# A decoder layer in fp32 split in two parts: in the first stage ScalarE makes the fp32 scaling of the input, and VectorE makes all lower parts of the index and query weights

## The chip, the cores and the metric

The kernel runs on one core of a Trainium2 chip. The metric is the device time of one execution in microseconds; the kernel before has a median of 1292.34 us over three runs (1291.21 to 1293.01). The engines are TensorE (PE in the profile, its weight loads PEld), VectorE (DVE), ScalarE (ACT) and GpSimd (POOL); SyncE (SP) issues every DMA.

## What is computed

One decoder layer over 1024 tokens and 1024 channels. What matters here is its beginning:

```python
mod = silu(c) @ w_mod + b_mod          # shift1, scale1, gate1, shift2, scale2, gate2
h = x * (1.0 + scale1) + shift1
proj = h @ w_in                        # columns [q | k | v | u | iq | ik | iw]
q, k, iq, ik = rope(q), rope(k), rope(iq), rope(ik)
score[t, s] = sum_h iw[t, h] * relu(iq[t, h] . ik[s])   # causal, s <= t
# the 256 keys of highest score are kept for each token; attention runs on those
```

Attention, a pooling branch, an output projection, two layer norms and a SwiGLU follow. The change does not touch them.

## The kernel before, in words

Every large matrix product is made with operands split in two: a higher part, which is the value rounded to the format that TensorE multiplies, and a lower part, which is the rest. Three products (high x high, high x low, low x high; `SPLITS`, line 293, in `mm_k`, line 295) stand for one. So each operand of 128x1024 costs two passes: `split` (line 276) has ScalarE copy the higher part out of a raw fp32 buffer and another engine subtract it from the raw buffer to give the lower part. That engine is VectorE unless `lo_eng` names GpSimd (`G`).

**First stage (loop over j, line 331).** The input is held with channels on partitions, in eight pieces of 128 channels, `xt` (128x1024, one column per token). For each piece j the loop loads two rows of `w_mod` (`wm`, two halves), has VectorE form scale1 and shift1 of its channels with two dot products of 128x1024 (`dot`, line 327) and two small additions, and then makes the two parts of h for these channels, `hT[j]`: ScalarE writes the higher part (line 349); a second instruction writes the scaled fp32 value back over `xt` (line 350); VectorE subtracts the one from the other for the lower part (line 351). At even j the next quarter of the index-query weights is split into `WS[j // 2]` (line 353). Then TensorE adds the products of this piece into seven open accumulators: index queries of token tiles 2 to 6 (`iq`, 15 matmuls a piece) and index keys and weights (`ik`, 6 matmuls a piece). Tile 7 is projected beside them by 24 matmuls named `pj`.

**Second stage, up to the scores.** ScalarE takes the index queries out of PSUM (`iq_take`), VectorE rotates tile 2 and the keys (`rope_tok(V, ...)`, line 456, and a rope on the transposed keys before it), and GpSimd rotates tiles 3 to 7 (line 466), three instructions of 128x512 a tile. Meanwhile the query weights take the place of the index-query weights in the same four buffers `WS[0..3]`: lines 457 to 463 split them, before with GpSimd for the lower parts of `WS[0]` and `WS[2]`, VectorE for `WS[1]` and `WS[3]`. TensorE projects query tile 0 with them (`pj`, four pieces of six matmuls; the first two pieces use `WS[0]` and `WS[1]`, the last two `WS[2]` and `WS[3]`), transposes the rotated tile 2 (`qT`) and the keys (`ikT`), and then starts the score products `lg` of tile 2. Scores of a tile are the eight heads' `lg`, a ReLU by ScalarE, and a weighted sum by VectorE (`score_X`). Query tile after query tile is projected between them. GpSimd rotates each projected query tile (`rope_V`) and masks the score tiles.

The raw weights go through a ring of three buffers (`RAW`, line 235). A load of the next raw piece waits until both parts of the old one have been made.

**What sets the order.** In these stages the framework's scheduler puts the instructions of each engine in an order from its own estimates; after this the instructions are kept in program order. Each engine works its list in order, so that an instruction that waits holds up all those behind it. SyncE's list of loads is in the order of the program.

Of the kernel before, what the change touches and what calls it, by code (L numbers as in the profile page):

```python
# [17 lines left out]
AF = mybir.ActivationFunctionType  # L18
ALU = mybir.AluOpType
# [54 lines left out]
def f_(ap):  # L74

    return ap.bitcast(F32)
# [110 lines left out]
def decoder_layer_kernel(  # L187
# [8 lines left out]
    V, A, G, T, SP = (Queue(tc, e, n, pinned, times) for e, n in  # L196
                      ((nc.vector, "V"), (nc.scalar, "A"), (nc.gpsimd, "G"), (nc.tensor, "T"), (nc.sync, "S")))
# [13 lines left out]
    def buf(where, off, n, name, dt=F32):  # L211
        return nc.alloc_sbuf_tensor_at(f"{name}_{where}{off}", [P, n], dt, offset=area[where] + 4 * off).ap()
# [21 lines left out]
    WS = [buf("W", k * 2048, 2048, "ws", F32R) for k in range(4)]  # L234
# [37 lines left out]
    def raw_slot():  # L272
        n_raw[0] += 1
        return RAW[(n_raw[0] - 1) % 3]

    def split(dst, raw, n, lo_eng=None):
        A.activation(dst[:, 0:n], raw, AF.Copy)
        (lo_eng or V).tensor_tensor(dst[:, n : 2 * n], raw, f_(dst[:, 0:n]), ALU.subtract)
# [6 lines left out]
    def hh(k, lo, t0, n):  # L285
        b = 1024 if lo else 0
        return hT[k][:, b + t0 : b + t0 + n]

    def ww(k, lo, c0, n):
        b = (1024 if lo else 0) + (k % 2) * 512  # L290
        return WS[k // 2][:, b + c0 : b + c0 + n]
# [3 lines left out]
    def mm_k(ps, lhs, rhs, ks):  # L295

        for k in ks:
            for m, (a, b) in enumerate(SPLITS):
                T.matmul(ps, lhs(k, a), rhs(k, b), start=(k == 0 and m == 0), stop=(k == KT - 1 and m == 2))
# [23 lines left out]
    def wikk(k, lo):  # L323
        b = (576 if lo else 0) + k * 72
        return wik[:, b : b + 72]

    def dot(wm, col):

        V.tensor_tensor_reduce(wm, wm, srow, 1.0, 0.0, ALU.mult, ALU.add, col)

    for j in range(KT):
        wm = wmr[j % 3]
        for hf in range(2):
            SP.dma_start(wm[:, hf * 1024 : (hf + 1) * 1024], wma_in[j][:, hf * 1024 : (hf + 1) * 1024])
        xt = xtr[j % 7]
        SP.dma_start(xt, xT_in[j])
        if j == 0:
            SP.dma_start(bcol, bcol_in)
        if j % 2 == 0:
            raw_iq = raw_slot()  # L340
            SP.dma_start(raw_iq, wiq_in[j // 2])
        if j == 0:
            SP.dma_start(wik_raw, wikw_in)
        mj = m1[:, 2 * j : 2 * j + 2]
        for hf in range(2):
            dot(wm[:, hf * 1024 : (hf + 1) * 1024], mj[:, hf : hf + 1])
        V.tensor_tensor(mj, mj, bcol[:, 2 * j : 2 * j + 2], ALU.add)
        V.tensor_scalar(mj[:, 0:1], mj[:, 0:1], 1.0, None, ALU.add)
        A.activation(hT[j][:, 0:1024], xt, AF.Identity, bias=mj[:, 1:2], scale=mj[:, 0:1])
        V.tensor_scalar(xt, xt, mj[:, 0:1], mj[:, 1:2], ALU.mult, ALU.add)  # L350
        V.tensor_tensor(hT[j][:, 1024:2048], xt, f_(hT[j][:, 0:1024]), ALU.subtract)
        if j % 2 == 0:
            split(WS[j // 2], raw_iq, 1024, G if j else V)
        if j == 0:
            split(wik, wik_raw, 576)
        for t in range(2, 7):
            mm_k(psq[t], lambda k, a: hh(k, a, t * P, P), lambda k, b: ww(k, b, 0, 512), [j])
        for c in range(2):
            mm_k(psk[c][0:72, :], lambda k, b: wikk(k, b), lambda k, a: hh(k, a, c * 512, 512), [j])
# [54 lines left out]
    raws = {}  # L414
# [40 lines left out]
                        float(np.float32(8.0 ** -0.5)), None, ALU.mult)  # L455
    rope_tok(V, iq_raw(2), iqtmp, 2)
    for kp in range(3):
        split(WS[kp], raws[kp], 1024, V if kp == 1 else G)
    raws[3] = raw_slot()
    SP.dma_start(raws[3], wq_in[3])  # L460
    for i in range(3, 7):
# [1415 lines left out]
```

## Time and profile before

| | |
|---|---|
| median of three runs | 1292.34 us |
| the profiled execution's own time | 1293.41 us |
| its span from first to last instruction | 1291.6 us |
| mean granted TensorE clock | 0.972 of full speed |
| busy: PE, DVE, ACT, POOL | 1200.3, 994.8, 654.5, 722.5 us |
| first stage: index-query products of the last piece end | about 63.5 us |
| first score product | 86.58 us |

Timeline rows read: start in us, length in us, engine, source line, operation, written tile <- read tiles, shapes, count, and in brackets the idle time of the engine just before and what ended it. Nearly all instructions have line L174, a helper that records every operation, so tiles tell them apart. A length of a merged row covers all its instructions. Matmul ends are modelled; the spacing of starts is the better measure, and PEld rows (weight loads, one per matmul) show it well.

### The profile page before, as it was taken

Reading aid. Unit: us, or ns where it says so; the run is one execution under the profiler, and the core shown is the slowest. Engines: PE = TensorE matmul, PEld = TensorE weight load, DVE = VectorE, ACT = ScalarE, POOL = GpSimd, SP = SyncE. Lnnn points to the kernel's source line nnn. Section 1 sums busy time; section 2 is a strip of 40 time slices with the busy share of each in tenths; the row PEclk is TensorE's granted clock in tenths of the full one; section 3 lists DMA queues with packets and bytes.
Section 4 is the critical chain, followed back from the end, with each engine's and each line's share of the span. In section 5 each row is a group of like instructions: output and inputs, shape, how many; then the busy total and the mean of one; then the engine's idle time right before and its main releaser. Section 6 shows DMA issues by size and latency. Waiting matters only on the chain.

```text
span 1291.6 us, 16411 instructions
## 1 busy us (share of the span) xinstructions
PE 1200.3 (93%) x5622; PEld 932.2 (72%) x5622; DVE 994.8 (77%) x1845; ACT 654.5 (51%) x1343; POOL 722.5 (56%) x510
## 2 busy tenths in 40 slices
PE   7979999999879999997799999999999999999996
PEld 6656565687646666886678787878888787878775
DVE  6758998877979866568687778687877777687798
ACT  3346878797668687265443333343433333333531
POOL 1383375657012355267666657483847566576848
PEclk9989999999958999999899999999999999999998
DMA  9510048521000016300111021201121110203112
GB/s 350 200 72 17 10 159 321 196 82 57 17 1 17 9 50 214 129 9 9 65 66 66 33 82 34 82 33 66 33 65 39 60 66 33 90 33 107 49 66 114
DMA packets 32460, 103.40 MB, mean 80 GB/s; under 512 B 3573, under 2 KB 3573, under 8 KB 28793
## 3 DMA queue, kind: packets, MB, share of 16 engines
q1 hardware_dynamic: 32376, 102.36, 22.5%
q8 instruction: 44, 0.72, 0.2%
q14 instruction: 40, 0.32, 0.1%
HBM read 92.90 MB, written 9.45 MB: 79 GB/s over the span
## 4 chain that ended last, share of the span: by engine, by line
PE 60%; DVE 18%; POOL 9%; issue 7%; ACT 5%; DMA 1%; SPq 0%; DVEq 0%; POOLq 0%; ACTq 0%
PE gu L174 24%; PE dn L174 14%; PE pj L174 5%; PE wo L174 4%; PE pair L174 3%; PE s L174 2%; PE pT L174 2%; PE o L174 2%; DVE act_W L174 2%; DVE score_X L174 2%; POOL wraw_R L174 2%; DVE junk_X L174 2%; PE lg L174 2%; DVE utmp_X L174 1%; POOL ws_W L174 1%
## 5 line engine op out<-in xcount | busy, mean ns | idle before, releaser
L174 PE MATMUL gu<-hr_H,wblk_T 128*128 128x512 f32 (+1 forms) x924 | 217.5, 388 | 6.1 <-ACT gtmp_V L174 2.7
L174 PE MATMUL gu<-hr_H,wblk_V 128*128 128x512 f32 (+1 forms) x924 | 215.8, 385 | 4.3 <-POOL wblk_V L174 2.1
L174 PEld LDWEIGHTS gu<-hr_H,wblk_T 128*128 128x128 f32 x924 | 172.2, 191 | 42.4 <-POOL wblk_T L174 3.6
L174 PEld LDWEIGHTS gu<-hr_H,wblk_V 128*128 128x128 f32 x924 | 169.9, 188 | 41.4 <-POOL wblk_V L174 4.2
L174 DVE TENSOR_TENSOR res_X<-res_X,dn 128x512 f32<-128x512 f32 (+1 forms) x253 | 159.0, 679 | 15.4 <-PE dn L174 15.3
L174 PE MATMUL pj<-ws_W,hT_H 128*128 128x512 f32 x456 | 117.3, 406 | 8.8 <-POOL ws_W L174 6.7
L174 POOL TENSOR_TENSOR wraw_R<-wraw_R 128x512 f32<-128x512 f32 x64 | 94.6, 1486 | 47.0 <-DVE wblk_T L174 23.7
L174 POOL TENSOR_TENSOR wraw_W<-wraw_W 128x512 f32<-128x512 f32 x60 | 86.9, 1456 | 59.6 <-DVE wblk_V L174 29.3
L174 POOL TENSOR_SCALAR sm_H<-sm_H,stat_X 128x1024 f32<-128x1024 f32 (+7 forms) x64 | 48.0, 764 | 124.1 <-DVE stat_X L174 96.0
L174 PEld LDWEIGHTS pj<-ws_W,hT_H 128*128 128x128 f32 x456 | 85.0, 192 | 33.2 <-POOL ws_W L174 7.0
L174 PE MATMUL dn<-wblk_T,act_W 128*128 128x512 f32 x324 | 78.8, 391 | 4.3 <-DVE act_W L174 4.3
L174 PE MATMUL dn<-wblk_V,act_W 128*128 128x512 f32 x324 | 78.5, 391 | 2.9 <-DVE act_W L174 2.5
L174 DVE TENSOR_SCALAR_CACHE_REDUCE junk_X<-keysD_T,colsD_X 128x1024 int16<-128x1024 int16 (+1 forms) x64 | 78.9, 1268 | 0.2
L174 ACT ACTIVATE wblk_V<-wraw_R 128x512 fp32r<-128x512 f32 x56 | 35.2, 629 | 81.2 <-POOL wraw_R L174 62.7
L174 POOL TENSOR_TENSOR ws_W<-raw_R,ws_W 128x1024 fp32r<-128x1024 f32 x17 | 44.3, 2625 | 53.4 <-ACT ws_W L174 53.4
L174 PEld LDWEIGHTS dn<-wblk_T,act_W 128*128 128x128 f32 x324 | 60.4, 188 | 18.9 <-DVE act_W L174 6.4
L174 PEld LDWEIGHTS dn<-wblk_V,act_W 128*128 128x128 f32 x324 | 60.4, 188 | 17.4 <-DVE act_W L174 4.2
L174 ACT ACTIVATE wblk_V<-wraw_W 128x512 fp32r<-128x512 f32 x53 | 33.1, 627 | 75.0 <-POOL wraw_W L174 56.4
L174 ACT ACTIVATE wblk_T<-wraw_W 128x512 fp32r<-128x512 f32 x56 | 35.0, 628 | 65.9 <-POOL wraw_W L174 50.2
L174 ACT ACTIVATE wblk_T<-wraw_R 128x512 fp32r<-128x512 f32 x52 | 32.5, 627 | 60.5 <-POOL wraw_R L174 44.5
L174 ACT ACTIVATE utmp_X<-gu 128x512 f32<-128x512 f32 x33 | 19.7, 598 | 74.7 <-PE gu L174 74.7
L174 ACT ACTIVATE sm_H<-sm_H,stat_X 128x1024 f32<-128x1024 f32 (+7 forms) x64 | 49.1, 771 | 16.7 <-DVE stat_X L174 16.5
(295 smaller groups left out, 2763.7 us busy)
## 6 DMA issues: line engine op xcount, KB each, us to landing
mset_K<-in_wmr_dram SPq DMA_DIRECT2D x16, 1024.0 KB, 5.6
wm_K<-in_wma_dram SPq DMA_DIRECT2D x16, 512.0 KB, 10.0
wraw_R<-in_wg_dram SPq DMA_DIRECT2D x6, 1024.0 KB, 4.8
wraw_R<-in_wd_dram SPq DMA_DIRECT2D x12, 512.0 KB, 3.7
wraw_W<-in_wup_dram SPq DMA_DIRECT2D x12, 512.0 KB, 3.7
wraw_R<-in_wup_dram SPq DMA_DIRECT2D x10, 512.0 KB, 3.6
wraw_W<-in_wg_dram SPq DMA_DIRECT2D x5, 1024.0 KB, 4.9
wraw_W<-in_wd_dram SPq DMA_DIRECT2D x10, 512.0 KB, 3.5
```

The lines of the kernel that those rows point to most:

```text
L174: ins_ = f(*a, **k)
```

## The change

Three lines of the program:

```diff
         A.activation(hT[j][:, 0:1024], xt, AF.Identity, bias=mj[:, 1:2], scale=mj[:, 0:1])
-        V.tensor_scalar(xt, xt, mj[:, 0:1], mj[:, 1:2], ALU.mult, ALU.add)
+        A.activation(xt, xt, AF.Identity, bias=mj[:, 1:2], scale=mj[:, 0:1])
         V.tensor_tensor(hT[j][:, 1024:2048], xt, f_(hT[j][:, 0:1024]), ALU.subtract)
         if j % 2 == 0:
-            split(WS[j // 2], raw_iq, 1024, G if j else V)
+            split(WS[j // 2], raw_iq, 1024)
...
     for kp in range(3):
-        split(WS[kp], raws[kp], 1024, V if kp == 1 else G)
+        split(WS[kp], raws[kp], 1024)
```

Eight instructions of 128x1024 go from VectorE to ScalarE, and five of 128x1024 go from GpSimd to VectorE (three for the index-query weights, two for the query weights). The scheduler then orders all engines of this stage anew. Behind the first score products the lists of all engines read the same as before, and SyncE's list of loads is the same from end to end.

On VectorE, in the first stage around piece j = 2 (`hT_H_63` is `hT[2]`, `xt_V_96` its input piece, `ws_W_70` is `WS[1]`, `wm_K` with ISA is a half of a dot product), before:

```order
L174 TENSOR_TENSOR hT_H_62<-xt_V_95,hT_H_62 128x1024
L174 TENSOR_TENSOR const_C_78<-const_C_78 128x2
L174 TENSOR_SCALAR const_C_78<-const_C_78 128x1
L174 TENSOR_SCALAR xt_V_96<-xt_V_96,const_C_78 128x1024
L174 ISA wm_K_91,const_C_78<-wm_K_91,srow_X_102 128x1024
L174 ISA const_C_78 128x1
L174 TENSOR_TENSOR hT_H_63<-xt_V_96,hT_H_63 128x1024
```

and now:

```order
L174 TENSOR_TENSOR hT_H_62<-xt_V_95,hT_H_62 128x1024
L174 TENSOR_TENSOR const_C_78<-const_C_78 128x2
L174 TENSOR_SCALAR const_C_78<-const_C_78 128x1
L174 ISA wm_K_91,const_C_78<-wm_K_91,srow_X_102 128x1024
L174 ISA const_C_78 128x1
L174 TENSOR_TENSOR ws_W_70<-raw_R_74,ws_W_70 128x1024
L174 TENSOR_TENSOR hT_H_63<-xt_V_96,hT_H_63 128x1024
```

The scaling of `xt` has left the list, and the lower part of the weights stands ahead of the lower part of `hT`.

On GpSimd, where the index queries are rotated (`iqraw_V`, `ptmp_C` with the table `gr_G`) and the lower part of `WS[2]` for the query weights (`ws_W_71` from `raw_R_73`) is made; `-` is before:

```order
-L174 TENSOR_TENSOR ws_W_69<-raw_R_74,ws_W_69 128x1024
-L174 TENSOR_TENSOR ptmp_C_455<-iqraw_V_447,gr_G_76 128x512
-L174 TENSOR_TENSOR iqraw_V_447<-iqraw_V_447,gr_G_76 128x512
-L174 TENSOR_TENSOR iqraw_V_447<-iqraw_V_447,ptmp_C_455 128x512
...
-L174 TENSOR_TENSOR ptmp_C_455<-iqraw_V_447,gr_G_76 128x512
-L174 TENSOR_TENSOR ws_W_71<-raw_R_73,ws_W_71 128x1024
```

Before, the lower part of `WS[2]` stood behind ten rotation instructions on GpSimd; now GpSimd's list holds the fifteen rotations alone.

On VectorE, at the end of the first stage and behind it (`ws_W_69` to `ws_W_72` are `WS[0]` to `WS[3]` with the query weights, `hT_H_68` is `hT[7]`), now:

```order
L174 TENSOR_TENSOR hT_H_68<-xt_V_94,hT_H_68 128x1024
L174 TENSOR_TENSOR ws_W_69<-raw_R_74,ws_W_69 128x1024
L174 TENSOR_TENSOR ws_W_70<-raw_R_75,ws_W_70 128x1024
L174 TENSOR_TENSOR iqtmp_V_448<-iqraw_V_447,gr_G_76 128x512
...
L174 TENSOR_TENSOR ikr_X_499<-ikr_X_499,ikt_X_500 128x256
L174 TENSOR_TENSOR ws_W_71<-raw_R_73,ws_W_71 128x1024
L174 TENSOR_TENSOR ws_W_72<-raw_R_74,ws_W_72 128x1024
L174 TENSOR_TENSOR ikE_K_554<-ikT_563,ikE_K_554 64x512
```

All four lower parts of the query weights stand on VectorE, two ahead of the rotations and two behind them; before, only `ws_W_70` and `ws_W_72` did, both behind the rotations.

## The prediction

> **What bounds the kernel now.** The page first: the matrix engine fills the chain of waits, so a stretch in which it stands still is where time can be had.
>
> ```profile
> PE 60%; DVE 18%; POOL 9%; issue 7%; ACT 5%; DMA 1%; SPq 0%; DVEq 0%; POOLq 0%; ACTq 0%
> ```
>
> Then the windows around the change (columns: window, its length, busy time and instructions of PE, PEld, DVE, ACT and POOL, granted clock, DMA share, GB/s).
>
> ```profile
> 30.00:40.00 10.00, 9.42 (x42) 7.16 (x42) 8.41 (x15) 3.44 (x3) 0.82 (x1) 1.00 1.03 411
> 60.00:70.00 10.00, 10.00 (x50) 7.86 (x49) 7.94 (x12) 6.61 (x11) 9.40 (x5) 1.00 0.16 52
> 70.00:80.00 10.00, 3.37 (x20) 2.39 (x18) 8.22 (x9) 5.05 (x9) 9.60 (x7) 0.90 0.15 52
> 80.00:90.00 10.00, 7.86 (x21) 5.91 (x21) 0.53 (x1) 0.96 (x2) 9.61 (x7) 0.59 0.29 106
> ```
>
> From 70 to 90 us POOL is full and PE mostly idle. The timeline names the reason.
>
> ```profile
> 72.47 1.43 PE L174 MATMUL pj<-ws_W,hT_H 128*128 128x512 f32 x5 [2.08 <-DVE ws_W L174]
> 79.75 2.33 POOL L174 TENSOR_TENSOR ws_W<-raw_R,ws_W 128x1024 fp32r<-128x1024 f32 x1
> 82.14 5.06 PE L174 MATMUL pj<-ws_W,hT_H 128*128 128x512 f32 x11 [6.70 <-POOL ws_W L174]
> 86.58 0.33 PEld L174 LDWEIGHTS lg<-ikE_K,qa_K 128*128 128x128 f32 x1
> 89.16 0.18 PEld L174 LDWEIGHTS lg<-ikE_K,ql_V 64*128 64x128 f32 x1 [0.35 <-issue]
> 90.16 0.42 DVE L174 TENSOR_SCALAR score_X<-relu_K,const_C 128x384 f32<-128x384 f32 x1 [9.63 <-ACT relu_K L174]
> ```
>
> PE waits 6.70 us for one lower part that POOL makes behind ten rotations, then runs 11 matmuls from 82.14 to 86.58, 0.40 us each. The Trainium skill (TensorE: Matmul & The Clock Gate, "What's actually happening") says that about 3.4 us of idling halves the clock; the trace agrees, with 0.59 granted there. DVE stands still for 9.63 us behind it. The first stage before that:
>
> ```profile
> 24.14 1.24 ACT L174 ACTIVATE hT_H<-xt_V,const_C 128x1024 fp32r<-128x1024 f32 x1 [3.42 <-DVE const_C L174]
> 25.28 1.05 ACT L174 ACTIVATE ws_W<-raw_R 128x1024 fp32r<-128x1024 f32 x1
> 25.41 0.81 DVE L174 TENSOR_SCALAR xt_V<-xt_V,const_C 128x1024 f32<-128x1024 f32 x1 [1.31 <-ACT hT_H L174]
> 26.41 3.18 POOL L174 TENSOR_TENSOR ws_W<-raw_R,ws_W 128x1024 fp32r<-128x1024 f32 x1 [24.39 <-ACT ws_W L174]
> 27.28 3.39 DVE L174 TENSOR_TENSOR hT_H<-xt_V,hT_H 128x1024 fp32r<-128x1024 f32 x1
> 40.06 3.38 DVE L174 TENSOR_TENSOR hT_H<-xt_V,hT_H 128x1024 fp32r<-128x1024 f32 x1
> 52.82 3.37 DVE L174 TENSOR_TENSOR hT_H<-xt_V,hT_H 128x1024 fp32r<-128x1024 f32 x1
> 59.88 1.23 DVE L174 TENSOR_TENSOR hT_H<-xt_V,hT_H 128x1024 fp32r<-128x1024 f32 x1
> ```
>
> DVE paces it, and POOL holds DVE up: a lower part takes DVE 1.23 alone, but 3.4 us in each of the three even pieces in which POOL makes a lower part at the same time (in the quoted pair POOL ends at 29.59 and DVE 1.1 us later, at 30.67). From j=2 to j=4 to j=6 the same instruction starts at 27.28, 40.06 and 52.82: 12.8 us for two pieces.
>
> **First stage on DVE.** Prices, start to start:
>
> ```profile
> 13.73 1.23 DVE L174 TENSOR_TENSOR hT_H<-xt_V,hT_H 128x1024 fp32r<-128x1024 f32 x1
> 14.87 1.22 DVE L174 TENSOR_TENSOR ws_W<-raw_R,ws_W 128x1024 fp32r<-128x1024 f32 x1
> 16.68 1.22 DVE L174 CUSTOM_DVE_ANT_0 wm_K<-wm_K,srow_X 128x1024 f32<-128x1024 f32 x1
> 17.82 1.22 DVE L174 CUSTOM_DVE_ANT_0 wm_K<-wm_K,srow_X 128x1024 f32<-128x1024 f32 x1
> ```
>
> A subtraction or a half dot product occupies DVE 1.14; ACT's scaling occupies ACT 1.14 (24.14 to 25.28), a copy 1.05; small additions cost 0.35 a piece. Two pieces now need four half dots, two lower parts of hT and one of the weights: 7 x 1.14 + 0.7 = 8.7 us. Two waits for ACT come on top. In an even piece ACT makes hT and the weights' copy (2.2) while DVE has one half dot (1.14): 1.1 of waiting. In an odd piece ACT makes hT and xt (2.3) while DVE has a half dot and small work (1.6): 0.7. That makes 10.5 us for two pieces, against 12.8. At the start the scaling on ACT delays the first lower part by 0.3 (1.14 for 0.81), and the weights' lower part now stands ahead of hT[2]'s: 13.73 + 0.3 + three subtractions (2.9) puts the next dots at 16.96; four half dots, hT[1]'s lower part, small work of 0.7 and 0.3 of waiting end at 23.7, ACT's three passes for j=2 (1.14 + 1.05 + 1.14) at 27.1. So hT[2]'s lower part starts at 27.1 (before 27.28), and hT[7]'s 2.5 pairs later, at about 53 instead of 59.88.
>
> **First stage on PE.** Two pieces are 42 matmuls. Their pace:
>
> ```profile
> 23.89 2.60 PEld L174 LDWEIGHTS iq<-ws_W,hT_H 128*128 128x128 f32 x12 [1.03 <-DVE hT_H L174]
> 26.53 1.30 PEld L174 LDWEIGHTS ik<-hT_H,wik_K 128*72 128x72 f32 x6
> 61.29 1.09 PE L174 MATMUL iq<-ws_W,hT_H 128*128 128x512 f32 x4
> 62.47 2.07 ACT L174 ACTIVATE iqraw_V<-iq 128x512 f32<-128x512 f32 x4 [2.51 <-PE iq L174]
> 64.49 0.84 PE L174 MATMUL pj<-ws_W,hT_H 128*128 128x512 f32 x3
> ```
>
> Twelve start in 2.64 us, 0.22 each; 42 need 9.3, and the order puts 15 pj matmuls between, 3.3 in all. So PE, with 10.4 a pair, is as late as DVE: hT[1]'s lower part is there at 23.2, 19 matmuls later PE has finished j=1 at 27.5, and it has 126 + 15 matmuls from there to the last index-key product, 31.3 us, to 58.8; before it was through at 64.5. Its last nine index-query matmuls begin at about 55.9 instead of 61.29, with hT[7] ready at 54. So ACT takes the queries out from 57.1 instead of 62.47: **5.4 us won**. DMA does not forbid it:
>
> ```profile
> 8.53 1.23 DVE L174 CUSTOM_DVE_ANT_0 wm_K<-wm_K,srow_X 128x1024 f32<-128x1024 f32 x1 [4.93 <-DMA wm_K<-in_wma_dram]
> ```
>
> ```profile
> wm_K<-in_wma_dram SPq DMA_DIRECT2D x16, 512.0 KB, 10.0
> ```
>
> The first dot has its two loads of 512 KB at 8.53; up to the last dot's half come 13.3 MiB more (15 halves, seven xt and four weight quarters of 512 KB, 0.3 for the key weights), at 411 GB/s 34 us, so 42 to 43 us. DVE asks for it at about 49.
>
> ACT's eight new passes (8 x 1.14 = 9.1 us) lie in its idle time: it is busy 3.44 of 10 us at 30 to 40. Without that cover they would lengthen each piece by up to 1.14. Queued behind them on ACT are the weights' copies, needed by PE a microsecond or more later.
>
> **The stall.** DVE makes the first two lower parts of the query weights right behind hT[7], 54.1 to 56.4, while nothing has been rotated yet. Then come the rotations and key work, as before:
>
> ```profile
> 63.09 0.82 DVE L174 TENSOR_TENSOR iqtmp_V<-iqraw_V,gr_G 128x512 f32<-128x512 f32 x1 [1.99 <-ACT iqraw_V L174]
> 70.13 4.51 DVE L174 TENSOR_TENSOR ws_W<-raw_R,ws_W 128x1024 fp32r<-128x1024 f32 x2
> 76.08 0.69 DVE L174 TENSOR_TENSOR ikE_K<-ikT,ikE_K 64x512 fp32r<-64x512 f32 x1 [1.44 <-ACT ikO_K L174]
> 79.12 1.41 DVE L174 TENSOR_TENSOR ql_V<-qT,qa_K 64x512 fp32r<-64x512 f32 x2 [0.23 <-ACT qa_K L174]
> ```
>
> From ACT's first take to the two lower parts were 70.13 - 62.47 = 7.66 us; 57.1 + 7.66 = 64.8. The other two lower parts take 4.5 us beside POOL's rotations, as that row shows: 69.3. PE has until then projected with the first two quarters, transposed queries and keys, and begun the third quarter; five matmuls behind 69.3 it can start `lg`, at 70.4 against 86.58. DVE's key parts (4 x 0.7) and query parts (1.41) end at 73.5, so `lg` with `ql` runs by 73.5 against 89.16: **15.7 us won in all**, 10.3 of it the stall. PE's waits on the way are 1 to 3 us; if one cooled the clock as at 82 us, twenty matmuls would cost 0.18 more each, 3.6.
>
> **POOL afterwards.** POOL's rotations of tiles 3 to 7 began at 63.63 and end at 88.75; without the 2.33 of weights they last 22.8, from 58.3 to 81.
>
> ```profile
> 63.63 1.45 POOL L174 TENSOR_TENSOR ptmp_C<-iqraw_V,gr_G 128x512 f32<-128x512 f32 x1 [0.26 <-ACT iqraw_V L174]
> 87.48 1.27 POOL L174 TENSOR_TENSOR iqraw_V<-iqraw_V,ptmp_C 128x512 f32<-128x512 f32 x1
> 91.19 3.22 DVE L174 SCALAR_TENSOR_TENSOR score_X<-relu_K,const_C,score_X 128x384 f32<-128x384 f32 x3 [0.61 <-ACT relu_K L174]
> 97.82 2.79 DVE L174 SCALAR_TENSOR_TENSOR score_X<-relu_K,const_C,score_X 128x384 f32<-128x384 f32 x4
> 100.36 1.41 POOL L174 TENSOR_TENSOR ptmp_C<-rope_V,gr_G 128x512 f32<-128x512 f32 x1 [7.09 <-ACT rope_V L174]
> ```
>
> That is 10.7 behind the first `lg`, where it was 2.2: POOL is 8.5 us later against the scores. Its 7.09 of idling at 100 takes most of that back. Meanwhile DVE's score sums meet POOL: 1.07 each with it, 0.70 without, so about ten of them cost 3.7 us of DVE, partly in its gaps. I charge 1.0 (bounds 0 and 8.5).
>
> **Sum.** 5.4 + 10.3 - 1.0 = 14.7. Behind the first scores all lists are as before and no load has a fixed time, so the shift passes to the end. From the profiled execution's 1293.41 that gives 1278.7, from the median 1292.34 (1.07 lower) 1277.6; I say 1278.
>
> **Rivals.**
>
> *ACT paces the first stage.* The same scaling is 0.81 on DVE and 1.24 for ACT's like row. The Trainium skill (ScalarE: Activation LUTs, "Rules for kernel authors") wants multiplications and additions on VectorE, not ScalarE; By it the eight moved passes cost 8 x 0.43 = 3.4 us where they are on the path. If ACT's passes did not overlap and stood in a row with DVE's, the stage would save nothing over today's 61 us, and only the stall goes: 1292.3 - 10.3 + 1 = about 1283. Against it: ACT's low busy share. 7%.
>
> *POOL's lateness is paid in full.* If score sums and masks wait for POOL by the whole 8.5: 1292.3 - 15.7 + 8.5 = 1285. Against it: POOL's 7.09 of idling. 6%.
>
> *The shift is lost later.* If DVE's search for the kept keys, which PE waits for later, did not start earlier, the time stays within a microsecond or two of 1292. Against it: that search is fed by the scores, and DVE idles before them. 4%.
>
> *Slower: a denser PE gets a lower clock.* The mean is 0.972.
>
> ```profile
> core 0: 1291.6 us, clock 0.972
> ```
>
> 60% of the span, 775 us, is PE's. A clock lower by 2.0% would cost 15.7 us and eat the whole gain; at 0.950 (2.3%) it costs 18 and gives 1295 to 1296. Against it: in 60 to 70 us PE is busy without a gap and the clock is 1.00. 4%.
>
> **How the numbers follow.** The forecast has 79%, with a range of its own of 1274 to 1282: all overlaps better than charged (nothing for POOL, 2 us less beside POOL's rotations in the 7.66) gives 1274.6; a cooled clock (3.6) gives 1281.6. The first two rivals, 1283 and 1285, belong into the range: 1273 to 1285. 0.2%, 2.6 us, is about what a measurement of this kernel can tell from no change. Faster by more: forecast and first two rivals, 0.92. Same: the third, 0.04. Slower: 0.04.
>
> **What would show it.** Right: lower parts of hT at 1.2 us throughout; the last index-query products near 56; first `lg` near 70, no PE wait over 3 us between 60 and 75, granted clock near 1.0 in 70 to 80; POOL's rotations ending near 81. Wrong in the first stage: DVE waits for ACT of over 1.5 us a piece and PE gaps there. Wrong in the sum: first `lg` at 70 but the layer's later stages shifted by less than 14, with waits of DVE or PE on POOL from 74 on.

## The result, and the profile after

The changed kernel takes 1278.17 us (median of 4 runs, 1276.36 to 1281.22) where the kernel before takes 1292.67 beside it (4 runs, 1291.21 to 1293.72). The ratio is 0.9891, 95% interval 0.9869 to 0.9913: faster by 1.1%, 14.5 us by the medians. The profiled execution took 1277.87 us with a span of 1276.1, 15.5 less than before. The forecast was 1278.0.

The shares of the chain that ended last come first again, then the cores' row.

```profile
PE 39%; DVE 7%; POOL 4%; issue 2%; ACT 1%; DVEq 0%; POOLq 0%; ACTq 0%
```

```profile
core 0: 1276.1 us, clock 0.972
```

These shares add up to 53%: the chain is lost halfway back and does not reach the first stage, so it can't be set beside the one before. The mean clock is the same 0.972 in the denser kernel. The windows do reach (window, length, busy time and instructions of PE, PEld, DVE, ACT, POOL, granted clock, DMA share, GB/s):

```profile
15.00:20.00 5.00, 4.23 (x9) 3.05 (x10) 4.93 (x10) 0.75 (x3) 0.00 (x0) 0.50 1.03 410
30.00:40.00 10.00, 10.00 (x46) 7.68 (x45) 8.01 (x13) 5.70 (x5) 0.00 (x0) 1.00 1.03 410
50.00:60.00 10.00, 10.00 (x46) 7.78 (x45) 5.19 (x9) 5.78 (x7) 0.22 (x1) 1.00 0.39 134
60.00:70.00 10.00, 9.16 (x51) 7.08 (x49) 9.97 (x12) 6.85 (x13) 9.53 (x7) 1.00 0.09 28
70.00:80.00 10.00, 9.15 (x36) 5.65 (x36) 9.21 (x11) 6.00 (x11) 9.53 (x7) 1.00 0.29 97
```

From 30 to 60 us PE has no gap (10.00 in the window of 40 to 50 us as well), and from 70 to 80 it is busy 9.15 where it was 3.37, with the clock at 1.00; from 60 to 70 DVE is full (9.97), POOL nearly. The clock of 0.50 at 15 to 20 comes back below. The stage now, from the timeline (start, duration, engine, instruction, and in brackets the idle time before it and what ended it):

```profile
26.19 1.23 DVE L174 TENSOR_TENSOR ws_W<-raw_R,ws_W 128x1024 fp32r<-128x1024 f32 x1 [1.12 <-ACT ws_W L174]
26.83 1.56 PE L174 MATMUL ik<-hT_H,wik_K 128*72 128x512 f32 x6
27.33 1.22 DVE L174 TENSOR_TENSOR hT_H<-xt_V,hT_H 128x1024 fp32r<-128x1024 f32 x1
53.62 1.22 DVE L174 TENSOR_TENSOR hT_H<-xt_V,hT_H 128x1024 fp32r<-128x1024 f32 x1 [2.59 <-ACT xt_V L174]
57.27 2.00 PEld L174 LDWEIGHTS iq<-ws_W,hT_H 128*128 128x128 f32 x9
58.60 2.07 ACT L174 ACTIVATE iqraw_V<-iq 128x512 f32<-128x512 f32 x4 [3.12 <-PE iq L174]
66.11 4.54 DVE L174 TENSOR_TENSOR ws_W<-raw_R,ws_W 128x1024 fp32r<-128x1024 f32 x2
```

The weights' lower part (26.19) stands ahead of `hT[2]`'s. Lower parts of `hT` take 1.22 in even pieces too, and `hT[7]`'s stands at 53.62, where it was 59.88; yet before it DVE waits 2.59 us for ACT. The first scores, and the last row of POOL's rotations:

```profile
64.25 2.97 PE L174 MATMUL pj<-ws_W,hT_H 128*128 128x512 f32 x12 [0.84 <-DVE const_C L174]
70.71 1.41 PE L174 MATMUL pj<-ws_W,hT_H 128*128 128x512 f32 x5 [0.55 <-DVE ws_W L174]
71.85 0.19 PEld L174 LDWEIGHTS lg<-ikE_K,qa_K 128*128 128x128 f32 x1 [0.16 <-ACT qa_K L174]
74.14 0.18 PEld L174 LDWEIGHTS lg<-ikE_K,ql_V 64*128 64x128 f32 x1 [0.74 <-DVE ql_V L174]
76.21 4.57 DVE L174 SCALAR_TENSOR_TENSOR score_X<-relu_K,const_C,score_X 128x384 f32<-128x384 f32 x3
82.01 1.28 POOL L174 TENSOR_TENSOR iqraw_V<-iqraw_V,ptmp_C 128x512 f32<-128x512 f32 x1
```

The wait of 6.70 us on POOL is gone; the largest of these PE waits is 0.84. First `lg` is 14.7 us earlier, `lg` with `ql` 15.0. How this shift passes through the program is seen in rows that group one instruction each (count, then shortest, median, longest duration in ns, then first and last start in us). Before, the query transposes and the loads of `mset_K` and of the residual input:

```profile
L174 PE MATMUL qT<-const_C,iqraw_V x24: 270/272/273, 73.7 to 142.5; 128*128 128x128 f32 x24
L168 SPq DMA_DIRECT2D mset_K<-in_wmr_dram x16: 327/328/419, 165.0 to 244.1; - x16
L168 SPq DMA_DIRECT2D res_X<-in_x_dram x8: 328/428/647, 483.9 to 500.3; - x8
```

and after:

```profile
L174 PE MATMUL qT<-const_C,iqraw_V x24: 270/272/273, 67.1 to 127.4; 128*128 128x128 f32 x24
L168 SPq DMA_DIRECT2D mset_K<-in_wmr_dram x16: 327/328/419, 149.9 to 228.9; - x16
L168 SPq DMA_DIRECT2D res_X<-in_x_dram x8: 328/428/541, 468.3 to 486.3; - x8
```

The last transpose is 15.1 us earlier, `mset_K` 15.1 to 15.2, the residual input 15.6 at its first load and 14.0 at its last, the end 15.5. So what is won by the first scores reaches the end, though the shift is down to 14.0 in between, and nothing is lost while POOL runs late.

### The profile page after: what moved, and what is told of

Same layout as the page of the kernel before. It is cut to its first block, busy times and chain, and to the rows that moved or that the text cites. A ratio compares the mean times of both kernels' runs of the same rounds, so it can differ in the third digit from the quotient of the medians.

```text
span 1276.1 us, 16417 instructions
## 1 busy us (share of the span) xinstructions
PE 1197.0 (94%) x5622; PEld 929.9 (73%) x5622; DVE 994.0 (78%) x1842; ACT 664.3 (52%) x1351; POOL 708.5 (56%) x505
## 4 chain that ended last, share of the span: by engine, by line
PE 39%; DVE 7%; POOL 4%; issue 2%; ACT 1%; DVEq 0%; POOLq 0%; ACTq 0%
PE gu L174 24%; PE dn L174 14%; DVE act_W L174 2%; POOL wraw_R L174 2%; DVE utmp_X L174 1%; POOL wraw_W L174 1%; DVE gtmp_V L174 1%; POOL wblk_V L174 1%; POOL wblk_T L174 1%; DVE wblk_T L174 1%; DVE hr_H L174 0%; POOL hr_H L174 0%; DVE wblk_V L174 0%; DVE res_X L174 0%; DVE stat_C L174 0%
## 5 line engine op out<-in xcount | busy, mean ns | idle before, releaser
L174 ACT ACTIVATE wblk_V<-wraw_R 128x512 fp32r<-128x512 f32 x56 | 35.2, 629 | 81.0 <-POOL wraw_R L174 62.6
L174 DVE SCALAR_TENSOR_TENSOR score_X<-relu_K,const_C,score_X 128x384 f32<-128x384 f32 (+5 forms) x42 | 54.2, 1290 | 5.0 <-ACT relu_K L174 1.4
```

What stands on the lines that cost most here:

```text
L174: ins_ = f(*a, **k)
```

## The experiments

The change has three parts: **A** the scaling on ScalarE (line 350), **B** the index weights' lower parts on VectorE (353), **C** the query weights' lower parts on VectorE (458). Edits are against the kernel before unless said otherwise. My theory: B frees VectorE, and what happens at the stall depends on the place that `WS[0]`'s and `WS[2]`'s lower parts get on GpSimd's list. The rival: each part brings a share of its own.

**B alone.**

```diff
-            split(WS[j // 2], raw_iq, 1024, G if j else V)
+            split(WS[j // 2], raw_iq, 1024)
```

> Only the lower parts of the index-query weights move from GpSimd to VectorE (line 353); scaling and query weights stay as before. In the new order GpSimd's list then holds the lower part of WS[2] ahead of all rotations. Theory 'places' (each microsecond goes to whoever stands behind the wrong instruction, so the stall at 75 to 82 us belongs to the place of WS[2]'s lower part on GpSimd and not to the line that names the engine): no 3.4 us subtractions in the first stage, two pieces in about 11.8 us, stage 3 us shorter, the stall gone too, first lg at 72 to 74 us, 1279 to 1282 us. Rival 'the parts add' (lines 350 and 353 own the first stage, line 458 alone owns the stall): first lg near 83, 1289 to 1290.

Measured: 1276.99 us (1276.46 to 1280.45), ratio 0.9885 (0.9868 to 0.9901). One part of three gives all of the gain. POOL's list behind the first stage:

```profile
53.65 3.33 POOL L174 TENSOR_TENSOR ws_W<-raw_R,ws_W 128x1024 fp32r<-128x1024 f32 x1 [51.62 <-ACT ws_W L174]
60.21 2.67 POOL L174 TENSOR_TENSOR ws_W<-raw_R,ws_W 128x1024 fp32r<-128x1024 f32 x1 [3.23 <-ACT ws_W L174]
62.85 1.74 POOL L174 TENSOR_TENSOR ptmp_C<-iqraw_V,gr_G 128x512 f32<-128x512 f32 x1
```

Both lower parts now stand ahead of all rotations, though line 458 is unchanged, and PE no longer waits for them. Why the scheduler places them there is not shown. First `lg` is at 71.28, and the time is 2 us below the range that the theory of places had given. The theory holds in kind; a share for each part does not.

**A and B.** Both diffs together, line 458 as before.

> Both edits of the first stage (lines 350 and 353), query weights as before with WS[0] and WS[2] on GpSimd. In the new order WS[2]'s lower part stands behind six rotations on GpSimd instead of ten. Theory 'places': first stage as in the changed kernel (last nine index-query matmuls near 57.3), WS[2] ready about 72, PE waits 1 to 3 us for it, first lg at 73 to 75, 1280 to 1281. Rival 'the parts add': 4 to 5 us for the first stage and the stall kept, 1288.

Measured: 1282.57 us (1281.05 to 1283.76), ratio 0.9919 (0.9905 to 0.9932): slower than B alone by 5.6 us with more of the change in it. The list says why:

```profile
68.23 2.14 POOL L174 TENSOR_TENSOR iqraw_V<-iqraw_V,ptmp_C 128x512 f32<-128x512 f32 x1
70.33 2.34 POOL L174 TENSOR_TENSOR ws_W<-raw_R,ws_W 128x1024 fp32r<-128x1024 f32 x1
72.73 3.94 PE L174 MATMUL pj<-ws_W,hT_H 128*128 128x512 f32 x11 [3.10 <-POOL ws_W L174]
```

`WS[2]`'s lower part stands behind six rotations here, PE waits 3.10 us, its next eleven matmuls take 0.34 each (3.74 us from the first to the first `lg` matmul), and `lg` starts at 76.05: the place as expected, the time 1.6 to 2.6 us above what I had said. In this execution two things were not in that sum. At 0.34 us, where the first stage's last ones took 0.227, the eleven matmuls take 1.2 more. And the first stage itself is 0.8 later than in the changed kernel (ACT takes the queries at 59.42 against 58.60), though its instructions are the same: PE's granted clock at 21 to 22 us is 0.50 here and 1.00 there.

**C alone.**

```diff
-        split(WS[kp], raws[kp], 1024, V if kp == 1 else G)
+        split(WS[kp], raws[kp], 1024)
```

> Only the lower parts of the query weights move to VectorE (line 458); first stage as before. Both theories: first stage unchanged (3.4 us subtractions stay, last nine index-query matmuls at 61.3), stall gone, granted clock near 1.0 in 75 to 90, first lg at 76, 1282 to 1283. A rival by which the first stage makes the whole gain: 1292.

Measured: 1284.86 us (1284.03 to 1286.45), ratio 0.994 (0.9927 to 0.9952). The first stage is as before, and the stall is gone, but `lg` starts at 79.23, three later than expected:

```profile
70.15 6.73 DVE L174 TENSOR_TENSOR ws_W<-raw_R,ws_W 128x1024 fp32r<-128x1024 f32 x3
```

I had counted two subtractions behind the rotations; in this order there are three, 2.24 us each beside POOL's rotations against 1.22 alone.

**B and C, the change without A.**

> The changed kernel with the scaling kept on VectorE (line 350 undone). My step: VectorE then has 8 x 0.81 us more and waits 1.3 us for ScalarE in even pieces, so two pieces take 11.8 us instead of 10.5; last nine index-query matmuls at 58.5 to 59.5 instead of 57.3, 1279.5 to 1281. Rival (scaling is cheaper on VectorE than on ScalarE, 0.81 against 1.24, so the move costs 3.4 us): faster than the changed kernel, 1275.

Measured: 1279.03 us (1277.5 to 1281.75), ratio 0.9894 (0.9878 to 0.991); first `lg` at 71.43. Not to be told from the whole change. So neither the rival holds, by which the kernel would be faster without ScalarE's longer passes, nor my own step, by which VectorE would have made it slower: `hT[7]`'s lower part stands at 53.47 (53.62 in the changed kernel), and ACT takes the first queries at 58.55 (58.60). In the windows of this kernel at 30 to 50 us DVE is nearly full and still PE has no gap:

```profile
30.00:40.00 10.00, 10.00 (x45) 7.55 (x44) 9.79 (x19) 3.44 (x3) 0.00 (x0) 1.00 1.03 410
40.00:50.00 10.00, 10.00 (x45) 7.67 (x44) 9.82 (x18) 3.45 (x3) 0.00 (x0) 1.00 0.87 325
```

So beside B the scaling's move does nothing that the times can tell: with it DVE goes from 9.8 us busy to between 8.0 and 8.5 and waits for ACT instead.

**A alone.**

```diff
-        V.tensor_scalar(xt, xt, mj[:, 0:1], mj[:, 1:2], ALU.mult, ALU.add)
+        A.activation(xt, xt, AF.Identity, bias=mj[:, 1:2], scale=mj[:, 0:1])
```

> Line 350 alone: the fp32 scaling goes to ScalarE, and every lower part stays where it was before (GpSimd: index weights of pieces 2, 4, 6 and query weights 0 and 2). In the kernel before VectorE paced the first stage, so here, other than beside the moved index weights, taking 0.81 us per piece off VectorE should help: a pair of pieces about 11.9 us where it was 12.8, ScalarE takes the queries at about 59.5 (before 62.47). The stall remains, since WS[2]'s lower part stands behind nine rotations on GpSimd's list, as it did behind ten: first score matmul at 83 to 84 where it was at 86.58. Theory (scaling counts only while VectorE paces): 1289 to 1291 us. Rival (the move does nothing in any setting, as it did beside the moved weights): 1292 to 1293 and first score matmul at 86 to 87. Rival by ScalarE's slower pass (1.24 for 0.81): 1295 to 1296.

Measured: 1290.44 us (11 runs, 1288.19 to 1292.51), ratio 0.9977 (0.9968 to 0.9986): 2.6 us by the medians, as the theory said, with first `lg` at 83.36. The move helps where POOL still makes index weights, but not all of the 3.2 us at `lg` is the first stage: ACT takes the queries at 60.71, 1.8 earlier (59.5 was expected), and the other 1.4 is about the length of one rotation on POOL: `WS[2]`'s lower part stands behind nine of them in place of ten. In the profiled execution, the slowest of the eleven with 1292.51, most of this is lost again: the first load of `mset_K` is 3.6 earlier than before and the last 0.5. Why is not shown. This run's timeline around `j` = 2:

```profile
26.32 2.41 POOL L174 TENSOR_TENSOR ws_W<-raw_R,ws_W 128x1024 fp32r<-128x1024 f32 x1 [24.29 <-ACT ws_W L174]
27.40 2.41 DVE L174 TENSOR_TENSOR hT_H<-xt_V,hT_H 128x1024 fp32r<-128x1024 f32 x1 [2.25 <-ACT xt_V L174]
78.92 5.06 PE L174 MATMUL pj<-ws_W,hT_H 128*128 128x512 f32 x11 [3.92 <-POOL ws_W L174]
```

The prediction's rows of before had 3.18 and 3.39 at this place. There POOL starts at 26.41, inside a half dot product that runs on DVE from 26.14; here DVE is still waiting for ACT's scaling when POOL starts, and POOL has its 2.4 us at once. In both kernels DVE's subtraction ends 1.08 us after POOL's (30.67 after 29.59, 29.81 after 28.73), as if it had only begun then. The Trainium skill (SBUF — State Buffer, "Who interferes with whom") has this as a rule: of a VectorE instruction with two SBUF inputs and a GpSimd instruction that reads SBUF, the later to issue blocks fully. Both traces agree, by these ends: in the six pairs of pieces 2, 4 and 6 of the two kernels DVE's end lies 1.08 or 1.09 behind POOL's. The stall remains, 3.92 us on POOL.

**A and C.**

> Lines 350 and 458 without 353: scaling on ScalarE, all query weights' lower parts on VectorE, the index weights' lower parts of pieces 2, 4 and 6 still on GpSimd. Beside e3_query_weights (1284.86, first score matmul at 79.23) this adds the scaling's move alone, with VectorE still held up by GpSimd in the first stage. Theory (scaling counts only while VectorE paces): 2.5 to 3.5 us earlier than e3_query_weights, first score matmul at 76 to 77, 1281 to 1283 us. Rival (the move does nothing in any setting): 1284 to 1286, first score matmul at 79.

Measured: 1283.49 us (1282.75 to 1286.17), ratio 0.993 (0.9917 to 0.9942). That is 1.4 under C alone, but the two intervals overlap, so by time it is undecided. In the trace ACT takes the queries at 60.7 where C alone has 62.6, and first `lg` is at 78.17, 1.1 earlier: short of the theory's 2 to 3, more than the rival's nothing. So the first stage gains about 2 us by the move, much as in A alone, and half of it is lost by the first score.

**POOL made later still.** The changed kernel, with four more products into scratch behind the index rotations; the output stays what it is.

```diff
     for i in range(3, NT):
         rope_tok(G, iq_raw(i), ptmp, i)
+    for _ in range(4):
+        G.tensor_tensor(ptmp, iq_raw(7), iq_raw(7), ALU.mult)
```

> The changed kernel with four more GpSimd products of 128x512 into a scratch tile after the five rotations of index queries: about 4 x 1.28 = 5.1 us more on GpSimd's list, the output unchanged, the other engines' lists unchanged. Theory (GpSimd's lateness costs nothing at this place; the charge of 1.0 us in the forecast was not needed): the first score matmul stays at 71.9, the span moves by less than 0.7 us, 1277.5 to 1279 us. Rival (what waits for the rotations is paid in full): the mask and the query rotations 5.1 us later, 1283 us.

Measured: 1279.52 us (1276.54 to 1280.65), ratio 0.9891 (0.9878 to 0.9905), the changed kernel's own ratio. Added work and what became of it:

```profile
83.95 5.18 POOL L174 TENSOR_TENSOR ptmp_C<-iqraw_V 128x512 f32<-128x512 f32 x4
89.20 1.36 POOL L174 TENSOR_TENSOR ptmp_C<-rope_V,gr_G 128x512 f32<-128x512 f32 x1
107.61 1.30 POOL L174 TENSOR_TENSOR ptmp_C<-rope_V,gr_G 128x512 f32<-128x512 f32 x1 [6.24 <-ACT rope_V L174]
```

```profile
L168 SPq DMA_DIRECT2D mset_K<-in_wmr_dram x16: 327/328/420, 151.3 to 230.6; - x16
```

The query rotations start 5.8 us later (83.37 in the changed kernel), and at 107 POOL is idle again for 6.24 us. First `lg` is at 72.47, 0.6 later already before the added work: here too the granted clock at 21 to 22 us is 0.50 where the changed kernel has 1.00, and PE is 0.6 later from `j` = 1 on. `mset_K` is 1.4 to 1.7 later. So 5.2 us on POOL cost about 0.8 to 1.1 by there. The span is 2.3 longer, more than the 0.7 that the theory allowed, but the times of the two kernels (medians 1.4 apart) can't be told apart; the rival's 5 us is out.

**A longer warm-up, looking for a faster kernel.** The changed kernel with one number changed.

```diff
-WARM = 66
+WARM = 104
```

> The changed kernel with 104 warm-up transposes in place of 66: they cover the stretch from 10.6 to about 15 us in which TensorE was idle, and the first index-query matmuls should run at 0.23 us each where they took 0.35 to 0.38 at a granted clock of 0.50. That is about 14 x 0.14 = 2 us earlier at that place. Theory (with VectorE relieved, TensorE's own chain from its first matmul sets the end of the first stage, but hT[1]'s lower part at 23.7 and hT[7]'s at 54.8 leave at most 1 us of it): last index matmul and first score matmul 0.5 to 1.0 us earlier (71.0 to 71.4), 1277.2 to 1277.8 us. Rival (VectorE still paces it): first score matmul at 71.9, no change. Rival (TensorE alone paces it): 2 us earlier, first score matmul at 69.9, 1276.2 us.

Measured: 1279.46 us (1278.67 to 1281.48), ratio 0.9897 (0.9882 to 0.9912): no gain. The warm-up's rows and what followed:

```profile
8.74 5.62 PE L174 MATMUL warm<-const_C 128*128 128x128 f32 x50
15.15 0.49 PE L174 MATMUL iq<-ws_W,hT_H 128*128 128x512 f32 x1 [0.79 <-ACT ws_W L174]
16.60 5.08 PE L174 MATMUL iq<-ws_W,hT_H 128*128 128x512 f32 x14 [0.96 <-DVE ws_W L174]
23.76 3.26 PE L174 MATMUL iq<-ws_W,hT_H 128*128 128x512 f32 x13 [0.22 <-DVE hT_H L174]
54.93 3.24 PE L174 MATMUL iq<-ws_W,hT_H 128*128 128x512 f32 x13 [0.24 <-DVE hT_H L174]
66.05 6.76 DVE L174 TENSOR_TENSOR ws_W<-raw_R,ws_W 128x1024 fp32r<-128x1024 f32 x3
```

The fourteen early matmuls still take 0.35 each on average (4.92 us to the next, at 21.52; 0.37 in the changed kernel), though PE now works up to 14.4 (11.5 in the changed kernel, not 10.6 as I had put it) and then waits only 0.79 and 0.96 us: the granted clock is 1.00 up to 17.8 us and 0.50 from 18.4 to 21. What they gain is worth nothing further on, since the next piece waits for `hT[1]`'s lower part: its thirteen weight loads begin at 23.75, in the changed kernel at 23.73. The last index-query matmul does end 1.5 us earlier (58.2, 59.7 in the changed kernel), but by another order of PE: no `pj` matmul stands ahead of it here, fifteen do in the changed kernel. And the scheduler, given another length for PE, put three query lower parts behind the rotations in place of two, and first `lg` came at 74.49, 2.6 later. My theory missed: it left the places out of account, the very thing that it held elsewhere. No kernel here beats B alone and the whole change beyond what the measurement can tell.

Across the kernels the first `lg` orders the times of the three parts: 86.58 before, 83.36 (A), 79.23 (C), 78.17 (A and C), 76.05 (A and B), and 71.85, 71.43, 71.28 (all; B and C; B). The times of the last three can't be told apart. The two variants of the changed kernel (72.47 and 74.49) have the same median, 1279.5, so a difference of 2 us at `lg` need not show in four runs.

## Why the prediction was right

The time was right to 0.2 us by the median, and the way to it holds in its main steps. That it was so close is luck: three terms of the sum were off by 0.8 to 1.5 us, they cancelled, and the runs themselves spread over 4.9 us.

*POOL holds DVE up in even pieces.* Right: without POOL's subtractions every lower part of `hT` takes 1.22, `hT[2]`'s stands at 27.33 (said: 27.1) and `hT[7]`'s at 53.62 (said: about 53). B alone does it. What the prediction left out is that PE also waited for POOL itself. In pieces 2, 4 and 6 of the kernel before, PE's weight loads stand until POOL has made the lower part of the index weights, as here in piece 4, and the changed kernel has no such wait:

```profile
42.41 0.75 PEld L174 LDWEIGHTS iq<-ws_W,hT_H 128*128 128x128 f32 x4 [1.80 <-POOL ws_W L174]
```

That part came late because POOL was held up by a dot product (above, A alone) and ACT's copy by DVE, so the account of DVE stands; but the last wait of PE in pieces 4 and 6 was for POOL and not for `hT`'s lower part.

*PE as late as DVE.* Right in kind, short in size: ACT takes the queries at 58.60, not at 57.1, so 3.9 us were won in the first stage and not 5.4. PE finished `j` = 1 at 28.39 where 27.5 was said. `hT[1]`'s lower part sets its start, as forecast, with 19 matmuls behind it:

```profile
23.73 2.84 PEld L174 LDWEIGHTS iq<-ws_W,hT_H 128*128 128x128 f32 x13 [0.41 <-DVE hT_H L174]
```

But it was there at 23.68 and not at 23.2, and a matmul follows its weight load by 0.2, which I had not counted. The granted clock of 0.50 in `j` = 0 cost nothing here, since PE then waited all the same; with A and B and with the later POOL it lasted longer, and PE went on 0.8 and 0.6 later without a wait for `hT[1]`. The rest is pace: nine matmuls start in 2.04 us, 0.227 each and not 0.222, which over 141 makes 0.7.

*The stall goes.* Right: from ACT's first take to the lower parts 7.51 us (said 7.66), two lower parts 4.54 (said 4.5), first `lg` 1.14 behind the last wait. `lg` with `ql` came at 74.14, only 0.6 behind the 73.5 said, since it needs the first of DVE's two query parts and I had waited for both. From the later first stage to here 15.0 were won in place of 15.7. One wait was not foreseen, 0.84 us until DVE had read the keys' transposes; it cost nothing that shows, since DVE's next two subtractions set the end.

*POOL's lateness, charged 1.0.* The charge was not needed. POOL's rotations end at 83.29 (said: 81), 11.4 behind the first `lg`, and DVE's sums do run slower beside them (4.57 for three, 1.52 each, where I had 1.07 from a row that had POOL beside it for only 2.1 of its 3.2 us); but the shift is 15.0 at the first `lg` with `ql` and 15.1 at `mset_K`. The run with 5.2 us more on POOL shows how much room is left there: about 0.8 to 1.1 us lost by `mset_K`.

*The sum.* Said: 5.4 + 10.3 - 1.0 = 14.7. By the trace: 3.9 in the first stage, 11.1 to the scores, nothing charged, 15.0, and 0.5 more by the end, which is well inside the spread between runs.

*What was argued for the parts.* The prediction told the change as one path through the program. It did not see that line 353 alone would give all of it, because it asked what each line costs and not where the scheduler would put the instructions that the line leaves in place. The scaling's move, which it counted as relief for DVE, is worth nothing that the times can tell in the changed kernel.

*The rivals.* That ACT paces the first stage is out: PE has no gap from 30 to 60 us, although DVE waits for ACT. The Trainium skill (ScalarE: Activation LUTs, "Rules for kernel authors") would keep such a scaling on VectorE; by time the runs can't tell the two places apart (1278.17 and 1279.03), as the pass is hidden on either engine; and where POOL still made index weights (A alone) the kernel was 2.6 us faster with it on ScalarE, in part by a place on POOL's list. POOL's lateness in full, and the shift lost later, are out by the shift of 14.0 to 15.6. The lower clock is out at 0.972.

## What to carry to other kernels

Where a scheduler sets the order, a moved instruction matters by what it does to the places of the others: read each engine's list of the new kernel, and cost the one wait that ends last there. Before moving several things at once, try each alone: one of three lines alone gave the whole gain, and two together were slower than that one. Taking work off an engine that was 98% busy gained nothing here, where another had no gaps beside it.

## What the runs showed of the hardware

- VectorE and GpSimd subtractions of 128x1024 fp32 do not share the time but follow each other: 1.22 us alone on DVE, 3.37 to 3.39 (before) and 2.37 to 2.41 (A alone) beside POOL's, each time ending 1.08 or 1.09 after POOL's.
- TensorE lost its clock after short waits: having worked up to 14.4 us and then waited 0.79 and 0.96 us, it had a granted clock of 1.00 up to 17.8 us and then, in the middle of matmuls without a gap, of 0.50 up to 21. Fourteen of them took 0.35 us each on average, against 0.227 later. What the clock goes by there was not tried.
- The stretch at half clock near the start lies differently in executions whose instructions up to there are the same: the granted clock is 0.50 from 13.8 to 20.4 us and 1.00 from 20.6 in the changed kernel, and still 0.50 at 21 to 22 with A and B and with the later POOL, where PE is 0.8 and 0.6 us later through the first stage.
